# Weight sums of the second FFN tied to its steps, two buffers for modulation rows, x's copies in two parts

## The chip, the cores and the metric

The kernel runs on one core of a Trainium2 chip. The metric is the device time of one execution in microseconds (us). TensorE (PE in the profile) multiplies matrices, VectorE (DVE) and ScalarE (ACT) work on tiles elementwise, GpSimd (POOL) helps with a few, and SyncE (SP) issues nearly all transfers (DMAs) from one queue that is worked through in order. Each engine takes its instructions in the order in which the program was laid out.

## The reference

One layer of a hybrid model on 512 tokens of width 1024, in float32. Three updates of x follow one another, each behind a norm that is scaled and shifted by rows computed from c:

```python
mod = jax.nn.silu(c) @ w_ada + b_ada
sh1, sc1, g1, sh2, sc2, g2, sh3, sc3, g3 = split(mod, 9)
u = rms_norm(x, ffn1_norm_g) * (1 + sc1) + sh1
x = x + 0.5 * g1 * swiglu(u, ffn1_w_in, ffn1_w_out)
u = rms_norm(x, mix_norm_g) * (1 + sc2) + sh2
...                     # mLSTM branch y_a, forgetting attention y_b, from u @ w_mix
merged = sigmoid(g_a) * (y_a @ w_branch_a) + sigmoid(g_b) * (y_b @ w_branch_b)
x = x + g2 * (merged @ w_out)
u = rms_norm(x, ffn2_norm_g) * (1 + sc3) + sh3
x = x + 0.5 * g3 * swiglu(u, ffn2_w_in, ffn2_w_out)
```

`swiglu(u, w_in, w_out)` is `(silu(a) * b) @ w_out` with `a, b` the halves of `u @ w_in`; the inner width is 2816. The change touches the update by `w_out`, the third norm, and the second FFN.

## The kernel before

**Splitting.** Every product is made of three matmuls (`mm3`, lines 108 to 110): each factor is split into a high part (line 89, on ACT) and a low part (line 91, on DVE). A weight tile is fetched into one of three `raw` buffers (`raw`, line 79, on SP), then split into one of four `wh` and four `wl` buffers. A buffer comes free when PE has used it, so weights are fetched and split a few tiles ahead of PE.

**The update by w_out.** `token_gemm` runs twice, once for each half of the 1024 columns, over four blocks of 128 tokens (0 to 3) and four slices of `w_out`. The first slices are multiplied for all blocks, the last two or three slices block by block, so that the blocks end one after another. `residual` gives each finished block to DVE: line 571 multiplies it by the modulation row, line 573 adds it to x, and line 209 (ACT) sums its squares. The modulation row is a tile of 128 x 512, fetched by `mod_bcast` (line 316) from a row in DRAM to all partitions; its tag `gb` has one buffer, so that the second half's row can be fetched only when the first half's last block is through.

**The third norm.** `norm_half` works on two token blocks at a time. `xnorm` (lines 229 to 237) makes the reciprocal root in ten small DVE instructions (lines 125 to 135), scales x, then PE transposes the tiles (line 260), and `u_from` (lines 245 to 247) makes the input of the next product. In the second half of the update, the norm of blocks 0 and 1 is written just ahead of block 3's matmuls, so that PE has block 2 and block 3 to do while the norm's small steps run. The same code, with the same tail of three slices, makes the second norm after the first FFN; there nothing else of a later stage lies beside it.

**The second FFN.** `ffn_in` goes through 22 columns j of 128 (columns 0 and 1 in `ffn_in_halves`, each in two halves of 256 tokens). A column takes two weight tiles. Its result is made by `pair_h`: SiLU on ACT (line 366), a multiply on DVE (line 372 for an even column, 378 for an odd one), and for each pair of columns some sums that serve a product of two-by-two blocks with seven products in place of eight. The weights of the second product need sums too. `pair_weights` makes them: 22 units, each a quarter of the pair's weights, loaded by two DMAs (line 425, tile `s`), four subtractions of 128 x 256 on DVE (lines 430 to 433), and a store to DRAM (line 435, `ws`). There are two tiles: one of tag `st` for even units, and for odd units the buffer that the last pair's `A1` will take. A unit's load, sums and store are written in three successive steps; a column has two steps, one between its two weight tiles and one at its end. An even unit and the odd unit behind it start every three steps. `pair_out` then multiplies, fetching `ws` again.

**What sets the order.** The program is written in the order of the stages, but a planner lays out each engine's instructions: it runs through the program on a clock of its own, and takes, among the instructions whose inputs and buffers are then ready, the one written first. An instruction can so land far ahead of its place when its inputs are early. `issue_after(i)` adds no wait: it only forbids that the instructions inside be placed ahead of `i` on that engine. The loads of `pair_weights` depend on nothing but a free buffer.

**Copies of x.** At the beginning of the second FFN eight DMAs (line 1271) copy x's eight tiles to DRAM (`x3_d`; the profile shows the name `x_d`), since the tiles' memory is used by the pairs. `pair_out` loads them again for the last update.

Of the kernel before, what the change touches and what calls it, by code (L numbers as in the profile page):

```python
# [11 lines left out]
F32 = mybir.dt.float32  # L12
# [8 lines left out]
P = 128  # L21
T = 512
NT = 4
D = 1024
# [19 lines left out]
MUL, ADD, SUB, MAX, MIN = ALU.mult, ALU.add, ALU.subtract, ALU.max, ALU.min  # L44


class Layer:
# [28 lines left out]
    def raw(self, shape, dmas):  # L76
        t = self.wp.tile(shape, F32, name=self.nm("raw"), tag="raw", bufs=3)
        for dst, src in dmas:
            self.nc.sync.dma_start(dst(t), src)
        return t  # L80

    def split(self, src, shape):
# [229 lines left out]
        return G, sh  # L312

    def mod_bcast(self, v, half, pool):
        t = pool.tile([P, 512], F32, name=self.nm("gb"), tag="gb", bufs=1)
        self.nc.sync.dma_start(t, self.mod_d[v:v + 1, half * 512:(half + 1) * 512].to_broadcast([P, 512]))
        return t

# [40 lines left out]
    def pair_h(self, ps_a, ps_b, j, c0, c1, hp, tp):  # L359


        nc = self.nc
        i, w, h0 = j // 2, c1 - c0, c0 // 256
        nh = w // 256
        s = self.tmp(tp, "sl")
        nc.scalar.activation(s[:, :w], ps_a[:, c0:c1], AF.Silu)
        hv = lambda t: t.rearrange("p (h t) -> p h t", t=256)
        if j % 2 == 0:
            if h0 == 0:

                self.E = tp.tile([P, 4, 256], F32, name=self.nm("E"), tag="E", bufs=1)
            nc.vector.tensor_tensor(self.E[:, 0:4:3, :] if nh == 2 else self.E[:, 3 * h0:3 * h0 + 1, :],
                                    hv(ps_b[:, c0:c1]), hv(s[:, :w]), op=MUL)
            return
        if h0 == 0:
            self.Ra[i], self.Rb[i] = self.pair_rest(i, hp, F32)
        Ra, Rb = self.Ra[i], self.Rb[i]
        nc.vector.tensor_tensor(Ra[:, h0:h0 + nh, :], hv(ps_b[:, c0:c1]), hv(s[:, :w]), op=MUL)
        if c1 < T:
            return  # L380
        E, V = self.E, nc.vector.tensor_tensor
        A1 = self.A1[i] = hp.tile([P, 6, 256], F32R, name=self.nm("A1"), tag=f"A{i}", bufs=1)
        V(E[:, 1, :], E[:, 3, :], Ra[:, 1, :], op=ADD)
        V(E[:, 2, :], E[:, 1, :], E[:, 0, :], op=SUB)
        nc.scalar.activation(A1[:, 0:3, :], E[:, 0:3, :], AF.Copy)
        V(A1[:, 3:6, :], E[:, 0:3, :], A1[:, 0:3, :], op=SUB)
        V(Rb[:, 0, :], E[:, 0, :], E[:, 3, :], op=SUB)
        V(Rb[:, 1, :], Ra[:, 0, :], E[:, 2, :], op=SUB)
# [22 lines left out]
    def pair_weights(self, w, hp, tp):  # L411


        nc = self.nc
        V = nc.vector.tensor_tensor
        NP = NJ // 2
        self.ws = [self.dp.tile([P, 4, 512], F32, name=self.nm("ws")) for i in range(NP)]
        ts = {}
        def load(u):
            i, c = u // 2, slice(u % 2 * 256, u % 2 * 256 + 256)  # L420

            t = ts[u] = hp.tile([P, 5, 256], F32, name=self.nm("s"), tag=f"A{NP - 1}", bufs=1) if u % 2 else                 tp.tile([P, 5, 256], F32, name=self.nm("s"), tag="st", bufs=1)
            for n in range(2):
                r = (2 * i + n) * P
                nc.sync.dma_start(t[:, 2 * n:2 * n + 2, :], w[r:r + P, :].rearrange("p (h n) -> p h n", h=2)[:, :, c])
        def sums(u):

            t = ts[u]
            s = lambda n: t[:, n, :]
            V(s(4), s(3), s(1), op=SUB)  # L430
            V(s(1), s(1), s(0), op=SUB)
            V(s(3), s(3), s(1), op=SUB)
            V(s(2), s(2), s(3), op=SUB)
        def store(u):
            nc.sync.dma_start(self.ws[u // 2][:, :, u % 2 * 256:u % 2 * 256 + 256], ts.pop(u)[:, 1:5, :])
        for h in range(3 * NP + 1):
            m, r = h // 3, h % 3
            for u, n in ((2 * m, r), (2 * m + 1, r - 1), (2 * m - 1, r + 2)):
                if 0 <= u < 2 * NP and 0 <= n < 3:
                    (load, sums, store)[n](u)  # L440
            yield
# [663 lines left out]
    def run(self):  # L1105
        nc, tc, A = self.nc, self.tc, self.A
# [2 lines left out]
        self.h_d = self.dp.tile([T, D], F32, name="h_d")  # L1109
        self.g_d = [self.dp.tile([P, T], F32, name=f"g_d{i}") for i in range(2 * NK)]  # L1110

        self.ntmp, self.xn_tiles, self.ffn_act = 5, self.xn_start, self.ffn_h
        with tc.tile_pool(name="f1t", bufs=1) as tp:
            self.consts(tp)
            with tc.tile_pool(name="st", bufs=1) as st:
# [114 lines left out]
                self.dump(f"ya_{m}", self.ya[m])  # L1230
                self.dump(f"yb_{m}", self.yb[m])

        self.ntmp, self.xn_tiles = 4, self.xn_branch
        with tc.tile_pool(name="br", bufs=1) as bp:
            self.mh = [bp.tile([P, T], F32R, name=f"mh{m}") for m in range(NK)]
            self.ml = [bp.tile([P, T], F32R, name=f"ml{m}") for m in range(NK)]

            sg = [bp.tile([P, T], F32, name=self.nm("sg"), tag="sg", bufs=2) for _ in range(2)]
            for m in range(2):
                for _ in self.gate(m, 0, None, sg[m]):  # L1240
                    pass
            self.split_y(self.ya, bp)
            ta = []
            for m in range(NK):
                ta.append(self.branch(m, 0, bp, yp.tile([P, T], F32, name=self.nm("ta"), tag="qk", bufs=16), sg[m] if m < 2 else None))
            self.split_y(self.yb, bp)
            for m in range(NK):
                t = self.branch(m, 1, bp, None)
                nc.gpsimd.tensor_tensor(t, t, ta[m], op=ADD)
                nc.scalar.activation(self.mh[m], t, AF.Copy)  # L1250
                nc.vector.tensor_tensor(self.ml[m], t, self.mh[m], op=SUB)
            self.x_tiles()
            self.x_load(self.x_d)
            lhs = lambda k: (self.mh[k], self.ml[k])
            self.ss_tile()
            self.token_gemm(lhs, NK, A["w_out"][0], 0, self.residual(0.5, 5, 0, bp))
            G3, sh3 = self.mod_cols(6, gain(R_N3))
            self.token_gemm(lhs, NK, A["w_out"][0], 1, self.residual(0.5, 5, 1, bp), 3, None,
                            lambda: self.norm_half(0, bp, G3, sh3))
            self.norm_half(1, bp, G3, sh3)  # L1260
# [4 lines left out]
        with tc.tile_pool(name="f2t", bufs=1) as tp, tc.tile_pool(name="f2h", bufs=1) as hp:  # L1265
            for k in range(NK):
                self.dump(f"u3_{k}", self.uh[k].bitcast(F32))
            x3 = self.dp.tile([T, D], F32, name="x3_d")
            for tb in range(NT):
                for h in range(2):  # L1270
                    nc.sync.dma_start(x3[tb * P:(tb + 1) * P, h * 512:(h + 1) * 512], self.x[tb][h])
            self.ffn_in_halves(A["ffn2_w_in"][0], 2, hp, tp)
            pw = self.pair_weights(A["ffn2_w_out"][0], hp, tp)
            step = lambda *_: next(pw, None)
            self.ffn_in(A["ffn2_w_in"][0], 2, hp, tp, step, step)
            for _ in pw:
                pass
            self.pair_out(A["ffn2_w_out"][0], 8, hp, tp, lambda: self.x_load(x3))


# [28 lines left out]
```

## Time and profile before

| | us |
|---|---|
| median of 3 runs | 1358.96 |
| lowest, highest | 1358.12, 1361.02 |
| the profiled execution | 1359.13 |
| its span | 1357.4 |
| PE busy | 1331.2 (98%) |
| DVE busy | 893.2 (66%) |
| ACT busy | 588.4 (43%) |

The stages around the change, in the profiled execution: the branches' last products end at 949.9; the update by `w_out` runs from there to 1002.8, with its second half from 972.6; the second FFN's first product follows, and the last column's multiply is at 1245.7; the second product runs to the end.

A line of a timeline gives the start and the duration in us, the engine, the line of the kernel, the operation, the tiles written and read, the shapes, the count, and in brackets for how long the engine stood idle before it and what ended that. A line of the waits gives the waiting engine, tile and line, what it waited for, the sum in us, the number of waits and the longest. A line of the windows gives a stretch, its length, busy time and instruction count of PE, PE's weight loads, DVE, ACT and POOL, then PE's granted clock (1.00 is full), the transfers' share and their rate in GB/s.

### The profile page before, as it was taken

How to read it: one execution, taken by the hardware profiler on the slowest of the kernel's cores; microseconds unless marked ns; L12 is line 12 of the kernel's file. 1: busy time of each engine (PE TensorE's matmuls, PEld its weight loads, DVE VectorE, ACT ScalarE, POOL GpSimd, SP SyncE). 2: the span in 40 equal slices, each digit the busy share in tenths (PEclk: the TensorE clock that was granted, in tenths of full speed). 3: DMA queues.
4: the chain of work that ended last, by engine and by line, in shares of the span. 5: the costliest groups of instructions: out<-in, count | busy, mean ns of one | idle time of the engine just before them, and what ended most of it. 6: DMA issues, size and time to landing. Idle time of an engine off the chain costs nothing.

```text
span 1357.4 us, 17796 instructions
## 1 busy us (share of the span) xinstructions
PE 1331.2 (98%) x6520; PEld 1116.0 (82%) x6520; DVE 893.2 (66%) x1661; ACT 588.4 (43%) x978; POOL 46.1 (3%) x71
## 2 busy tenths in 40 slices
PE   7999999999999999999999999999999999999997
PEld 6788887887889888988888888888788888888886
DVE  6866666656558777986686876446577655434776
ACT  4532333313236755556565675333253222323642
POOL 2000000000011101000000000002010000000000
PEclk9999999999999999999999999999989999999999
DMA  9676556666534424444243442464558875434575
GB/s 288 188 224 189 179 184 202 217 194 201 187 86 107 131 85 136 123 116 132 59 140 89 132 129 77 117 198 142 177 170 258 262 229 176 123 93 140 168 249 164
DMA packets 245691, 219.30 MB, mean 162 GB/s; under 512 B 12706, under 2 KB 206914, under 8 KB 245604
## 3 DMA queue, kind: packets, MB, share of 16 engines
q1 hardware_dynamic: 245124, 218.09, 53.6%
q8 instruction: 51, 0.84, 0.2%
q14 instruction: 36, 0.29, 0.1%
q0 software_dynamic: 416, 0.06, 0.0%
q10 hardware_dynamic: 64, 0.02, 0.0%
HBM read 194.47 MB, written 23.66 MB: 161 GB/s over the span
## 4 chain that ended last, share of the span: by engine, by line
PE 88%; DVE 6%; ACT 3%; DMA 2%; issue 1%; SPq 0%; DVEq 0%; ACTq 0%
PE g L110 23%; PE g L108 23%; PE g L109 23%; PE t L110 4%; PE t L108 4%; PE t L109 4%; PE g L693 2%; PE t L1037 2%; PE t L1007 1%; DVE wl L91 1%; DMA s<-in_ffn_w_out_dram 1%; PE t L978 1%; PE t L979 1%; PE t L693 1%; DVE fq L957 1%
## 5 line engine op out<-in xcount | busy, mean ns | idle before, releaser
L89 ACT ACTIVATE wh<-raw 128x1024 fp32r<-128x1024 f32 x236 | 244.3, 1039 | 401.5 <-PE g L109 141.7
L91 DVE TENSOR_TENSOR wl<-raw,wh 128x1024 fp32r<-128x1024 f32 x236 | 289.6, 1229 | 164.4 <-ACT wh L89 147.7
L108 PE MATMUL g<-uh,wh 128*128 128x512 f32 (+2 forms) x984 | 370.3, 377 | 0.5 <-ACT wh L89 0.5
L110 PE MATMUL g<-uh,wl 128*128 128x512 f32 (+2 forms) x984 | 369.4, 376 | 1.1 <-DVE wl L91 1.1
L109 PE MATMUL g<-ul,wh 128*128 128x512 f32 (+2 forms) x984 | 369.3, 376 | 0.0
L110 PEld LDWEIGHTS g<-uh,wl 128*128 128x128 f32 (+1 forms) x984 | 184.7, 188 | 35.7 <-DVE wl L91 1.7
L108 PEld LDWEIGHTS g<-uh,wh 128*128 128x128 f32 (+1 forms) x984 | 184.7, 188 | 33.9 <-ACT wh L89 0.9
L109 PEld LDWEIGHTS g<-ul,wh 128*128 128x128 f32 (+1 forms) x984 | 184.9, 188 | 33.1 <-POOL ul L247 0.2
L108 PE MATMUL g<-wh,uh 128*128 128x512 f32 (+1 forms) x320 | 111.9, 350 | 0.0
L110 PE MATMUL g<-wh,ul 128*128 128x512 f32 (+1 forms) x320 | 111.1, 347 | 0.0
L109 PE MATMUL g<-wl,uh 128*128 128x512 f32 (+1 forms) x320 | 111.0, 347 | 0.0
L284 DVE SCALAR_TENSOR_TENSOR acc<-raw,ccol,acc 128x1024 f32<-128x1024 f32 x49 | 62.8, 1282 | 13.0 <-DMA raw<-in_w_ada_dram 12.2
L108 PEld LDWEIGHTS g<-wh,uh 128*128 128x128 f32 x320 | 60.5, 189 | 7.8 <-DVE tk L892 0.5
L110 PEld LDWEIGHTS g<-wh,ul 128*128 128x128 f32 x320 | 60.5, 189 | 7.8
L109 PEld LDWEIGHTS g<-wl,uh 128*128 128x128 f32 x320 | 60.5, 189 | 7.3
L430 DVE TENSOR_TENSOR s<-s 128x256 f32<-128x256 f32 x22 | 9.3, 425 | 62.8 <-DMA s<-in_ffn_w_out_dram 53.3
L108 PE MATMUL g<-yh,wh 128*128 128x512 f32 x128 | 50.4, 394 | 0.0
L110 PE MATMUL g<-yh,wl 128*128 128x512 f32 x128 | 50.2, 392 | 0.0
L109 PE MATMUL g<-yl,wh 128*128 128x512 f32 x128 | 49.7, 388 | 0.0
L989 ACT ACTIVATE S<-S,mn 128x128 f32<-128x128 f32 (+1 forms) x64 | 35.6, 558 | 18.5 <-DVE mn L981 9.5
L108 PE MATMUL g<-wh,hh 128*128 128x512 f32 x88 | 35.0, 398 | 0.0
L110 PE MATMUL g<-wh,hl 128*128 128x512 f32 x88 | 34.9, 397 | 0.0
(319 smaller groups left out, 2087.1 us busy)
## 6 DMA issues: line engine op xcount, KB each, us to landing
raw<-in_ffn_w_in_dram SPq DMA_DIRECT2D x82, 512.0 KB
raw<-in_w_ada_dram SPq DMA_DIRECT2D x56, 512.0 KB
raw<-in_w_mix_dram SPq DMA_DIRECT2D x48, 512.0 KB
raw<-in_ffn_w_out_dram SPq DMA_DIRECT2D x33, 512.0 KB
s<-in_ffn_w_out_dram SPq DMA_DIRECT2D x44, 256.0 KB
ws<-s SPq DMA_DIRECT2D x22, 512.0 KB
ar<-in_w_ada_dram SPq DMA_DIRECT2D x32, 256.0 KB
raw<-in_w_mix_dram SPq DMA_DIRECT2D x32, 256.0 KB
```

The lines of the kernel that those rows point to most:

```text
L89: nc.scalar.activation(hi, src, AF.Copy)
L91: nc.vector.tensor_tensor(lo, src, hi, op=SUB)
L108: mm(ps, lh, rh, start=start, stop=False)
L109: mm(ps, lh, rl, start=False, stop=False)
L110: self.last_mm = mm(ps, ll, rh, start=False, stop=stop)
L284: nc.vector.scalar_tensor_tensor(acc, r, self.ccol[:, k:k + 1], acc, op0=MUL, op1=ADD)
L693: mm = nc.tensor.matmul(acc_ps[b], (wl if p == 1 else wh)[:, b % 2, s], self.ul[k] if p == 2 else self.uh[k], start=k == 0 and p == 0, sto ...
L957: nc.vector.scalar_tensor_tensor(lo, b[own, :], gc[own, :], d[own, :], op0=MUL, op1=SUB)
L978: nc.tensor.matmul(ps[:, :w], q[:, s], k[:, :w], start=True, stop=False)
L979: nc.tensor.matmul(ps[:, :w], q[:, s], kl[:, :w], start=False, stop=True)
L989: nc.scalar.activation(S[:, ws], S[:, ws], AF.Exp, scale=-1.0, bias=m, accum_out=sm[:, qb:qb + 1])
L1037: nc.tensor.matmul(po[:, q0:], vt[:, kb, i, :], Px[:, o:o + T - q0], start=n == 1, stop=n == 8)
```

## The change

It has three parts.

1. In `pair_weights` the two loads of a unit are placed behind the last weight load written before them (`last_raw`, noted by `raw`) on SP, and the four subtractions behind the last multiply of a column written before them (`last_mul`, noted by `pair_h`) on DVE.
2. The modulation rows of the update by `w_out` take the tag `sg`, whose two buffers the branches use before; the tag `gb` no longer exists in that stage. The first FFN keeps `gb` with one buffer.
3. The four copies of x's left half are written behind the first half of the update, the other four where all eight were.

```diff
@@ raw
-            self.nc.sync.dma_start(dst(t), src)
+            self.last_raw = self.nc.sync.dma_start(dst(t), src)
@@ mod_bcast
-        t = pool.tile([P, 512], F32, name=self.nm("gb"), tag="gb", bufs=1)
+        tag, n = self.gb_tag
+        t = pool.tile([P, 512], F32, name=self.nm("gb"), tag=tag, bufs=n)
@@ pair_h
-            nc.vector.tensor_tensor(self.E[:, 0:4:3, :] if nh == 2 else self.E[:, 3 * h0:3 * h0 + 1, :],
+            self.last_mul = nc.vector.tensor_tensor(self.E[:, 0:4:3, :] if nh == 2 else self.E[:, 3 * h0:3 * h0 + 1, :],
...
-        nc.vector.tensor_tensor(Ra[:, h0:h0 + nh, :], hv(ps_b[:, c0:c1]), hv(s[:, :w]), op=MUL)
+        self.last_mul = nc.vector.tensor_tensor(Ra[:, h0:h0 + nh, :], hv(ps_b[:, c0:c1]), hv(s[:, :w]), op=MUL)
@@ pair_weights
-                nc.sync.dma_start(t[:, 2 * n:2 * n + 2, :], w[r:r + P, :].rearrange("p (h n) -> p h n", h=2)[:, :, c])
+                with self.tc.issue_after(self.last_raw.ins):
+                    nc.sync.dma_start(t[:, 2 * n:2 * n + 2, :], w[r:r + P, :].rearrange("p (h n) -> p h n", h=2)[:, :, c])
...
-            V(s(4), s(3), s(1), op=SUB)
-            V(s(1), s(1), s(0), op=SUB)
-            V(s(3), s(3), s(1), op=SUB)
-            V(s(2), s(2), s(3), op=SUB)
+            with self.tc.issue_after(self.last_mul.ins):
+                V(s(4), s(3), s(1), op=SUB)
+                V(s(1), s(1), s(0), op=SUB)
+                V(s(3), s(3), s(1), op=SUB)
+                V(s(2), s(2), s(3), op=SUB)
@@ run
-        self.ntmp, self.xn_tiles, self.ffn_act = 5, self.xn_start, self.ffn_h
+        self.ntmp, self.xn_tiles, self.ffn_act, self.gb_tag = 5, self.xn_start, self.ffn_h, ("gb", 1)
...
-        self.ntmp, self.xn_tiles = 4, self.xn_branch
+        self.ntmp, self.xn_tiles, self.gb_tag = 4, self.xn_branch, ("sg", 2)
...
             self.token_gemm(lhs, NK, A["w_out"][0], 0, self.residual(0.5, 5, 0, bp))
+            self.x3_d = self.dp.tile([T, D], F32, name="x3_d")
+            def x_spill(h):
+                for tb in range(NT):
+                    nc.sync.dma_start(self.x3_d[tb * P:(tb + 1) * P, h * 512:(h + 1) * 512], self.x[tb][h])
+            x_spill(0)
...
-            x3 = self.dp.tile([T, D], F32, name="x3_d")
-            for tb in range(NT):
-                for h in range(2):
-                    nc.sync.dma_start(x3[tb * P:(tb + 1) * P, h * 512:(h + 1) * 512], self.x[tb][h])
+            x_spill(1)
...
-            self.pair_out(A["ffn2_w_out"][0], 8, hp, tp, lambda: self.x_load(x3))
+            self.pair_out(A["ffn2_w_out"][0], 8, hp, tp, lambda: self.x_load(self.x3_d))
```

## The prediction

> **What bounds the kernel now.** I read the page's busy times first, then what TensorE (PE) waited for, then VectorE (DVE) and PE in order of time where the longest late wait lies.
>
> ```profile
> span 1357.4 us, 17796 instructions
> PE 1331.2 (98%) x6520; PEld 1116.0 (82%) x6520; DVE 893.2 (66%) x1661; ACT 588.4 (43%) x978; POOL 46.1 (3%) x71
> ```
> ```profile
> PE t L178 <- DMA rowsC<-in_b_ada_dram: 5.8, 1, 5.8
> PE g L693 <- ACT uh L658: 5.6, 8, 1.4
> PE t L260 <- DVE xn L236: 3.0, 1, 3.0
> ```
>
> PE is the bound: it idles 1357.4 - 1331.2 = 26.2 us. The first two waits belong to the start of the kernel, which the diff does not touch. The third, 3.0 us, is the only long one after it: PE stands before the transposes of the third norm. No edit here can gain more than that wait and what hangs on it. The work around it, first DVE, then PE:
>
> ```profile
> 972.88 0.42 DVE L430 TENSOR_TENSOR s<-s 128x256 f32<-128x256 f32 x1 [4.57 <-DMA s<-in_ffn_w_out_dram]
> 983.53 0.69 DVE L571 SCALAR_TENSOR_TENSOR rs<-g,gb 128x512 f32<-128x512 f32 x1 [2.46 <-DMA gb<-mod_d]
> 987.55 0.42 DVE L430 TENSOR_TENSOR s<-s 128x256 f32<-128x256 f32 x1 [3.33 <-DMA s<-in_ffn_w_out_dram]
> ...
> 989.75 0.68 DVE L571 SCALAR_TENSOR_TENSOR rs<-g,gb 128x512 f32<-128x512 f32 x1
> 990.46 0.69 DVE L573 TENSOR_TENSOR x<-x,rs 128x512 f32<-128x512 f32 x1
> 992.01 0.16 DVE L230 SCALAR_TENSOR_TENSOR v<-ss,v 128x2 f32<-128x2 f32 x1 [0.85 <-ACT rs L209]
> 994.19 0.49 DVE L236 TENSOR_SCALAR xn<-x,rq 128x512 f32<-128x512 f32 x1
> ```
> ```profile
> 986.43 0.40 PE L110 MATMUL g<-wh,ml 128*128 128x512 f32 x1
> ...
> 990.63 0.40 PE L110 MATMUL g<-wh,ml 128*128 128x512 f32 x1
> ...
> 991.33 0.39 PE L110 MATMUL g<-wh,ml 128*128 128x512 f32 x1
> 994.73 1.11 PE L260 MATMUL t<-ident,xn 128*128 128x128 f32 x4 [3.01 <-DVE xn L236]
> ```
>
> What the reader is to see: PE finishes block 1 of w_out's second half at 986.43 + 0.40 = 986.83. DVE could take its update (L571) at once, but stands at L430, the first weight sum of an FFN that has not begun, until that sum's slice lands at 987.55. Sums and older updates go first, so block 1's update starts at 989.75, 2.9 us late. From its second step (990.46) to the transposes (994.73) the chain is 4.27 us without a hole: square on ACT, rsqrt steps from 992.01, xn at 994.19. PE has three matmuls of block 3 after block 2 and then nothing.
>
> The gap has a second price. The windows of one microsecond, whose column after POOL is the granted clock:
>
> ```profile
> 993.00:994.00 1.00, 0.00 (x0) 0.00 (x0) 0.83 (x6) 0.00 (x0) 0.00 (x0) 0.85 0.30 111
> 994.00:995.00 1.00, 0.27 (x1) 0.27 (x2) 0.96 (x3) 0.81 (x2) 0.00 (x0) 0.50 0.20 20
> 999.00:1000.00 1.00, 1.00 (x5) 0.81 (x4) 1.00 (x3) 1.00 (x4) 0.12 (x1) 0.50 0.00 0
> 1000.00:1001.00 1.00, 1.00 (x5) 0.82 (x4) 1.00 (x4) 1.00 (x3) 0.73 (x1) 0.73 0.00 0
> 1001.00:1002.00 1.00, 1.00 (x6) 0.81 (x5) 1.00 (x4) 1.00 (x3) 0.85 (x1) 1.00 0.00 0
> ```
>
> From 994.73 to 1000 PE works at half clock and loses 5.27 x 0.50 = 2.6 us, in the next microsecond 0.27: 2.9 us. Idle and clock together cost 5.9 us.
>
> **The change part by part.**
>
> *Sums tied behind their own steps on DVE* (L430 to L433). 22 units of four subtractions stay, but none can be issued before the last multiply of the second FFN that was written ahead of it. The first sum so falls behind FFN 2's third column, after the whole stage above. In that stage DVE then has nothing of L430 before block 1's update: L571 at 986.83 + 0.03, L573 0.71 later (989.75 to 990.46) at 987.57, transposes 4.27 later at 991.84. PE is done with its three matmuls at 991.72. Idle 0.1 us in place of 3.0. A gain of 2.9, and with no gap the clock should hold: 2.9 more, 5.8 at most.
>
> A check from the kernel itself: the second norm, after the first FFN's update, runs the same code without sums beside it. Its update of block 1, its transposes and the transposes of its other half, with the last row for the third norm:
>
> ```profile
> 392.25 0.69 DVE L571 SCALAR_TENSOR_TENSOR rs<-g,gb 128x512 f32<-128x512 f32 x1 [2.78 <-PE g L110]
> ...
> 397.19 0.66 PE L260 MATMUL t<-ident,xn 128*128 128x128 f32 x4
> ...
> 412.23 1.94 PE L260 MATMUL t<-ident,xn 128*128 128x128 f32 x16
> ...
> 1011.97 1.94 PE L260 MATMUL t<-ident,xn 128*128 128x128 f32 x16
> ```
> ```profile
> 397.00:398.00 1.00, 0.93 (x7) 0.69 (x6) 1.00 (x3) 1.00 (x2) 0.00 (x0) 1.00 0.00 0
> ```
>
> There the clock is 1.00 through the transposes. From block 1's sum being ready to the other half's transposes the twin takes 412.23 - 392.25 = 19.98 us; here it is 1011.97 - 986.86 = 25.11. The difference is 5.1. Between 5.1 and 5.8 I take 5.1, because the twin holds the small waits that a denser DVE brings.
>
> [...]
>
> *Where the sums go, and what they cost there.* FFN 2's columns come 10.89 us apart:
>
> ```profile
> 1169.60 0.69 DVE L372 TENSOR_TENSOR E<-g,sl 128x512 f32<-128x512 f32 x1 [3.36 <-PE g L110]
> 1180.49 0.69 DVE L378 TENSOR_TENSOR Ra<-g,sl 128x512 f32<-128x512 f32 x1 [3.37 <-PE g L110]
> ```
> ```profile
> 1133.06 0.43 DVE L430 TENSOR_TENSOR s<-s 128x256 f32<-128x256 f32 x1 [3.55 <-DMA s<-in_ffn_w_out_dram]
> 1144.78 0.43 DVE L430 TENSOR_TENSOR s<-s 128x256 f32<-128x256 f32 x1 [6.58 <-DMA s<-in_ffn_w_out_dram]
> ```
> ```profile
> 1025.00:1060.00 35.00, 35.00 (x168) 29.49 (x167) 22.73 (x42) 10.85 (x13) 0.00 (x0) 1.00 0.89 273
> ```
> ```profile
> DVE s L430 <- DMA s<-in_ffn_w_out_dram: 37.9, 12, 7.1
> ```
>
> One buffer needs 1144.78 - 1133.06 = 11.7 us from one unit's sums to the next (store, load, sums). A buffer comes round every three steps, two steps to a column, so its ties lie one and two columns apart in turn: 10.9 and 21.8 us. In the long turn nothing waits; in the short one DVE may wait 11.7 - 10.9 = 0.8 us for the slice. Eleven such waits make some 9 us, against the 37.9 us (longest 7.1) that DVE waits at L430 from 1025 to 1245 today, during which PE is 35.00 of 35.00 us busy in the fullest window. What is queued behind a waiting sum is the split of a weight (L91). Its slack:
>
> ```profile
> 1174.80 1.06 ACT L89 ACTIVATE wh<-raw 128x1024 fp32r<-128x1024 f32 x1 [4.38 <-PE g L109]
> 1175.90 1.23 DVE L91 TENSOR_TENSOR wl<-raw,wh 128x1024 fp32r<-128x1024 f32 x1 [4.01 <-ACT wh L89]
> ```
>
> The split starts when PE leaves one of four weight buffers and is done 2.33 us later (1177.13); three other weights of 10.89 / 2 = 5.44 us lie ahead, so DVE may be late by 16.3 - 2.3 = 14.0 us before PE feels it. Cost zero, bounds 0 and the rival below.
>
> *Loads tied on SP* (L425, two of 256 KB a unit, and the store L435 behind its sums). The same 44 loads and 22 stores are issued, each behind a weight load of FFN 2. They leave the stretch of the third norm and go past FFN 2's weight loads, with the slack just named. The last sums now come behind the multiply four columns before the last one:
>
> ```profile
> 1202.25 0.69 DVE L378 TENSOR_TENSOR Ra<-g,sl 128x512 f32<-128x512 f32 x1 [3.37 <-PE g L110]
> ...
> 1245.70 0.69 DVE L378 TENSOR_TENSOR Ra<-g,sl 128x512 f32<-128x512 f32 x1 [2.06 <-PE g L110]
> ```
> ```profile
> 1215.82 0.43 SPq L79 DMA_DIRECT2D raw<-ws  x1
> ```
>
> So at 1202, before the first read of the summed weights (1215.82, which wants the first unit only) and before the last pair at 1245.70 takes the odd units' buffer. Cost zero.
>
> *Modulation rows in two buffers* (L316, tag "sg"). The second row now need not wait for the first; the 2.46 us wait at 983.53 goes. It alone is worth nothing: that update was through by 985, ahead of block 1's end at 986.83. Both rows now take buffers that the branches hold:
>
> ```profile
> 953.23 0.68 DVE L1251 TENSOR_TENSOR ml<-sg,mh 128x512 fp32r<-128x512 f32 x1
> 964.10 0.69 DVE L571 SCALAR_TENSOR_TENSOR rs<-t,gb 128x512 f32<-128x512 f32 x1 [0.48 <-PE t L110]
> 977.40 0.87 SPq L316 DMA_DIRECT2D gb<-mod_d  x1
> ```
>
> Such a row takes 983.53 - 977.40 = 6.1 us to land at worst. The last branch frees its buffer at 953.91, so even that one lands by 960, ahead of the first use at 964.10. Zero, and up to the 4 us of margin could be lost if SP is held.
>
> *x's copies in two parts* (L1271). Eight transfers as before, the first four merely written earlier; they become ready only with the updates, and PE waits for none of them. Zero.
>
> *Sum.* 1357.4 - 5.1 = 1352.3 us of span. The profiled execution took 1359.13, 1.73 around its span, and the median is 1358.96, 0.17 less: 1352.3 + 1.73 - 0.17 = 1353.9 us, a gain of 0.38%.
>
> **The rivals.**
>
> *The hole stays.* The planner lays the order anew, and block 2's update may land ahead of the small rsqrt steps. Block 2 ends at 990.63 + 0.40 = 991.03; its two steps of 0.71 end at 992.45, the rsqrt steps and xn start then instead of at 987.57 + 992.01 - 990.46 = 989.12, and the transposes 994.73 - 992.01 = 2.72 later, at 995.2: an idle gap of 3.4 us and the half clock again. Nothing is gained: 1359. Against it: the twin has its block 2 update behind the first xn. Chance 0.10.
>
> *The clock falls anyway.* If half clock belonged to the sparse transposes and not to the gap, only the 2.9 us of idle come back: 1356.1. The twin's clock of 1.00 speaks against it. Chance 0.03. [...]
>
> *The late sums starve PE.* DVE waits at L430, behind its multiply, with weight splits behind it; from 14.0 us late PE idles, and a gap like today's costs 5.9 us with its clock. Two of them, less the gain of 5.1, give 1358.96 + 11.8 - 5.1 = 1365.7, slower. It decides where a wait at L430 passes 14 us, or several pile up within one column; for it: the sums' whole load moves into the one stretch with transfers at a share of 0.89, and each chain store, load, sums starts from a multiply. Against: the longest such wait today is 7.1 us. Chance 0.15.
>
> **How the numbers follow.** Forecast 0.72, clock rival 0.03, no gain 0.10, starved 0.15. A measurement of this kernel tells about 0.2%, 2.7 us (its runs spread over 2.9). Faster by more: 0.72 + 0.03 = 0.75; within: 0.10; slower: 0.15. The forecast's own range is 1353.0 to 1355.5. For eight in ten it reaches over the clock rival to the case without gain: 1352.8 (the 5.8 ceiling and 0.3 of spread) to 1359.4.
>
> **What would show it.** Right: no L430 before the first 128x512 multiply of FFN 2; PE's wait at L260 under 0.5 us; clock 1.00 from transposes to FFN 2; the two halves' transposes as far apart as in the twin; waits at L430 short and PE waiting for no wl there; the span's gain all between the w_out matmuls and FFN 2's start. Wrong: a gap before L260 of over 2 us, or PE waiting for wl or wh after 1020.

## The result and the profile after

| | before | after |
|---|---|---|
| median of 8 runs, us | 1358.78 | 1354.65 |
| lowest, highest | 1357.82, 1361.02 | 1354.13, 1357.03 |
| the profiled execution | 1359.13 | 1354.64 |
| its span | 1357.4 | 1352.9 |

The ratio is 0.9972, with a 95% interval from 0.9961 to 0.9983: faster by 4.13 us or 0.3%. The forecast was 1353.9; the kernel takes 0.75 us more. In the new program's line numbers the sums are L434 to L437, their loads L427 and store L439, the update L575 and L577, the column multiplies L373 and L379.

First the page's busy times and the waits of PE, whose columns are those of the table before (sum, number, longest):

```profile
span 1352.9 us, 17800 instructions
PE 1328.6 (98%) x6520; PEld 1113.0 (82%) x6520; DVE 887.8 (66%) x1661; ACT 589.4 (44%) x978; POOL 46.0 (3%) x71
```
```profile
PE g L697 <- ACT uh L662: 5.6, 8, 1.4
PE t L178 <- DMA rowsC<-in_b_ada_dram: 5.6, 1, 5.6
```

The wait of 3.0 us at L260 is gone, and what leads the list now belongs to stages that the change doesn't touch. PE is busy 2.6 us less (1331.2 before) and idle 1352.9 - 1328.6 = 24.3 us, 1.9 less than before. DVE's timeline of the changed kernel through the third norm, with a column multiply far behind it:

```profile
986.98 0.69 DVE L575 SCALAR_TENSOR_TENSOR rs<-g,gb 128x512 f32<-128x512 f32 x1 [2.78 <-PE g L110]
...
991.44 0.49 DVE L236 TENSOR_SCALAR xn<-x,rq 128x512 f32<-128x512 f32 x1
994.82 1.00 DVE L246 TENSOR_SCALAR uf<-t,G,sh 128x256 f32<-128x256 f32 x2 [1.31 <-ACT uh L245]
...
1197.78 0.69 DVE L379 TENSOR_TENSOR Ra<-g,sl 128x512 f32<-128x512 f32 x1 [3.37 <-PE g L110]
```

DVE waits for PE now and not for a slice: block 1's update starts as soon as its sum is there. PE's timeline of the same kernel from the transposes to the second FFN (the 128x256 matmuls are its first), the start of the second FFN in the kernel before, and windows of the changed kernel (PE with the number of its matmuls, its weight loads, DVE, ACT, POOL, granted clock, transfers):

```profile
991.98 0.66 PE L260 MATMUL t<-ident,xn 128*128 128x128 f32 x4
...
996.91 0.39 PE L109 MATMUL g<-wl,mh 128*128 128x512 f32 x1
997.14 0.40 PE L110 MATMUL g<-wh,ml 128*128 128x512 f32 x1
997.37 0.28 PE L108 MATMUL g<-uh,wh 128*128 128x256 f32 x1
997.50 0.28 PE L109 MATMUL g<-ul,wh 128*128 128x256 f32 x1
...
1001.66 0.39 PE L110 MATMUL g<-uh,wl 128*128 128x256 f32 x1 [0.16 <-DVE wl L91]
...
1007.08 1.95 PE L260 MATMUL t<-ident,xn 128*128 128x128 f32 x16
```
```profile
1002.54 0.40 PE L110 MATMUL g<-wh,ml 128*128 128x512 f32 x1
1002.77 0.28 PE L108 MATMUL g<-uh,wh 128*128 128x256 f32 x1
```
```profile
991.00:992.00 1.00, 0.86 (x5) 0.38 (x3) 0.89 (x5) 0.56 (x1) 0.00 (x0) 1.00 0.00 0
995.00:996.00 1.00, 1.00 (x6) 0.77 (x5) 1.00 (x3) 1.00 (x3) 0.10 (x1) 1.00 0.06 21
998.00:999.00 1.00, 1.00 (x11) 1.00 (x10) 1.00 (x3) 1.00 (x2) 0.56 (x1) 1.00 0.00 0
1150.00:1215.00 65.00, 65.00 (x289) 53.81 (x288) 34.33 (x62) 17.92 (x22) 0.00 (x0) 1.00 0.71 216
```

The clock is 1.00 at every place where it was 0.50 (in every window from 990 to 1006). Behind the norm's transposes PE works, up to 997.37, on block 3 of `w_out`, whose matmuls of 128x512 start every 0.23 us (996.91, 997.14); at half clock, in the kernel before, they started 0.42 us apart (999.49, 999.91). The second FFN's first matmul comes at 997.37 in place of 1002.77. In the ten microseconds behind it DVE is the fuller engine, 1.00 busy in every window from 995 to 1004, and PE waits once for a weight's split (1001.66). Further on in the second FFN PE is busy without a hole, though the sums and their transfers have moved there. DVE's waits at the sums and SP's at the stores, between 1020 and 1280:

```profile
DVE s L434 <- DMA s<-in_ffn_w_out_dram: 3.7, 4, 1.8
```
```profile
SPq L439 <- DVE s L437: 45.1, 15, 6.3
```

**Where the time came from.** Set beside the rows of before, the first xn of the norm comes at 991.44 in place of 994.19, 2.75 us earlier. The second FFN's first matmul comes 5.40 us earlier, the transposes of the other half 4.89 (1007.08 in place of 1011.97). The column multiply at 1197.78 stood at 1202.25: 4.47 us earlier, and this distance stays to the end (4.49 between the two profiled executions). So 2.75 us are won ahead of the first xn and 2.65 between it and the second FFN, and 0.93 of that is given back behind its first matmul, which leaves 1.72 us behind the first xn. This last part can be read as one number in any kernel: the stretch from the first xn to that column multiply took 1202.25 - 994.19 = 208.06 us before and takes 1197.78 - 991.44 = 206.34 us now. The experiments below use it, since it leaves out whatever an execution lost earlier.

### The profile page after: what moved, and what is told of

It reads as the page before. It is cut to its first block, busy times and chain, and to the rows that moved or that the text cites. A ratio compares the mean times of both kernels' runs of the same rounds, so it can differ in the third digit from the quotient of the medians.

```text
span 1352.9 us, 17800 instructions
## 1 busy us (share of the span) xinstructions
PE 1328.6 (98%) x6520; PEld 1113.0 (82%) x6520; DVE 887.8 (66%) x1661; ACT 589.4 (44%) x978; POOL 46.0 (3%) x71
## 4 chain that ended last, share of the span: by engine, by line
PE 86%; DVE 7%; ACT 3%; DMA 2%; issue 1%; SPq 0%; DVEq 0%; ACTq 0%
PE g L110 22%; PE g L108 22%; PE g L109 22%; PE t L110 4%; PE t L108 4%; PE t L109 4%; PE g L697 2%; PE t L1041 2%; PE t L1011 1%; DVE wl L91 1%; PE t L982 1%; PE t L983 1%; PE t L697 1%; DVE fq L961 1%; DMA h_d<-hn 1%
## 5 line engine op out<-in xcount | busy, mean ns | idle before, releaser
L108 PE MATMUL t<-wh,hh 128*128 128x512 f32 x88 | 34.8, 396 | 0.0
```

Source lines behind the costliest of these rows:

```text
L108: mm(ps, lh, rh, start=start, stop=False)
```

## The experiments

Four questions: which part of the change carries the gain, whether the sums cost anything where they now stand, what the parts other than the ties do alone, and what the 1.72 us behind the first xn consist of. Ratios are to the kernel before on the same chip.

| kernel | median us | before | ratio, 95% interval |
|---|---|---|---|
| both ties alone | 1355.09 | 1358.61 | 0.9976, 0.9967 to 0.9986 |
| the sums' tie alone | 1354.42 | 1358.61 | 0.9969, 0.9958 to 0.9981 |
| the loads' tie alone | 1355.57 | 1358.61 | 0.9978, 0.9970 to 0.9987 |
| both ties alone, from unit 4 | 1354.47 | 1358.61 | 0.9969, 0.9956 to 0.9981 |
| no ties, the other two parts | 1363.89 | 1358.56 | 1.0036, 1.0022 to 1.0050 |
| the two buffers alone | 1363.31 | 1358.56 | 1.0034, 1.0021 to 1.0048 |
| x's copies in two parts alone | 1358.95 | 1358.56 | 1.0004, 0.9995 to 1.0013 |
| before, with fill | 1359.53 | 1358.56 | 1.0007, 0.9998 to 1.0016 |
| both ties alone, from unit 6 | 1358.79 | 1359.39 | 0.9994, 0.9986 to 1.0003 |
| ties from unit 6, with fill | 1357.86 | 1359.39 | 0.9994, 0.9985 to 1.0003 |
| ties from unit 6, copies in two parts | 1359.04 | 1358.66 | 1.0008, 0.9999 to 1.0016 |
| the sums' tie from unit 6 | 1358.59 | 1358.66 | 0.9995, 0.9987 to 1.0004 |

### The ties, together and one by one

Both ties without the other two parts (against the changed kernel):

```diff
-        self.ntmp, self.xn_tiles, self.gb_tag = 4, self.xn_branch, ("sg", 2)
+        self.ntmp, self.xn_tiles, self.gb_tag = 4, self.xn_branch, ("gb", 1)
-            x_spill(0)
...
-            x_spill(1)
+            for tb in range(NT):
+                for h in range(2):
+                    nc.sync.dma_start(self.x3_d[tb * P:(tb + 1) * P, h * 512:(h + 1) * 512], self.x[tb][h])
```

> Both ties of the weight sums, but the modulation rows in one buffer and x's copies in one part, as before. Theory (the early sums on VectorE are the whole cause): VectorE meets no L430-type sum before block 1's update, the transposes wait for under 0.3 us, the clock stays at 1.00; 1354.7 us, as the full change. Rival (the second buffer for the modulation row carries part of the gain, since block 0's update waited 2.46 us for it): 1355.5 to 1357 us, with a wait for the row ahead of block 1's update.

Measured 1355.09. The interval overlaps that of the whole change almost entirely, so beside the ties the other two parts add nothing that can be told.

The sums' tie alone (against the kernel before; the lines that note the multiply in `pair_h` are left out here):

```diff
-            V(s(4), s(3), s(1), op=SUB)
...
+            with self.tc.issue_after(self.last_mul.ins):
+                V(s(4), s(3), s(1), op=SUB)
...
```

> Only the four subtractions are tied; the loads of the first two units still go out early on SP. Theory (what stands in VectorE's queue is the cause): 1354.7 us, no gap at the third norm. Rival (SP's early loads and stores, standing ahead of weight loads and copies, cost PE as well): at least 1 us of the gain missing, 1355.7 to 1357 us, and a wait of PE for a weight.

The loads' tie alone (against the kernel before; the line that notes the load in `raw` is left out here):

```diff
-                nc.sync.dma_start(t[:, 2 * n:2 * n + 2, :], w[r:r + P, :].rearrange("p (h n) -> p h n", h=2)[:, :, c])
+                with self.tc.issue_after(self.last_raw.ins):
+                    nc.sync.dma_start(t[:, 2 * n:2 * n + 2, :], w[r:r + P, :].rearrange("p (h n) -> p h n", h=2)[:, :, c])
```

> Only the loads are tied; the sums are free but need their slice. Theory: the sums can't be ready before the second FFN and are laid out behind the norm, 1354.7 us. Rival (without the tie on VectorE the sums move ahead of the second FFN's own multiplies and hold weight splits there): a wait of PE for a split in the second FFN and 1356 us or more.

Measured 1354.42 and 1355.57: either tie alone brings nearly all of it. A sum that may not be issued early does no harm, and a sum whose load is issued late isn't taken early by the planner either. The loads' tie is also the test of the rival that starves PE, since it leaves the sums where the planner puts them. DVE's waits at the sums between 1025 and 1245, and the window, in the kernel with the loads' tie alone:

```profile
DVE s L434 <- DMA s<-in_ffn_w_out_dram: 31.6, 13, 4.9
```
```profile
1025.00:1245.00 220.00, 220.00 (x972) 182.17 (x971) 119.25 (x195) 60.60 (x73) 0.00 (x0) 1.00 0.66 200
```

DVE waits 31.6 us for slices, up to 4.9 us at a time, and PE is busy 220.00 of 220.00 us. So it isn't the length of these waits that counts but where they stand; the likely reason is the prediction's slack of 14.0 us for a split. Ahead of 1025 a free sum likely did cost something: one stands on DVE ahead of the norm's second half, with a wait of 0.76 us at 1008.64, and the stretch from the first xn is 206.95 us, 0.6 more than in the changed kernel, in this one execution.

### Units 0 to 3 left free

Both ties hold from unit 4 on, without the other two parts; the first four units, two for each pair of columns and each with half of its weights, are placed as before (against the kernel with both ties alone):

```diff
-                with self.tc.issue_after(self.last_raw.ins):
+                with self.tc.issue_after(self.last_raw.ins) if u >= 4 else nullcontext():
...
-            with self.tc.issue_after(self.last_mul.ins):
+            with self.tc.issue_after(self.last_mul.ins) if u >= 4 else nullcontext():
```

> Units 0 to 3 stay untied, so the sums of units 0 and 2 still stand in the first half of the update by w_out and make VectorE wait there (5.16 and 4.57 us before); from unit 4 on all is tied. Theory (only a wait that ends later than block 1's result reaches PE, and that is unit 4's alone): 1354.7 us, the whole gain. Rival (each early wait costs its share): one of three waits is gone, a third of the gain, about 1357.4 us.

Measured 1354.47. The early waits of DVE at units 0 and 2 (in the kernel before 4.57 us at 972.88, here 4.10) cost nothing that can be told; the gain hangs on the units from 4 on.

### The two other parts without the ties

No ties, but the two buffers and the copies in two parts (against the changed kernel):

```diff
-                with self.tc.issue_after(self.last_raw.ins):
-                    nc.sync.dma_start(t[:, 2 * n:2 * n + 2, :], w[r:r + P, :].rearrange("p (h n) -> p h n", h=2)[:, :, c])
+                nc.sync.dma_start(t[:, 2 * n:2 * n + 2, :], w[r:r + P, :].rearrange("p (h n) -> p h n", h=2)[:, :, c])
...
-            with self.tc.issue_after(self.last_mul.ins):
+            with nullcontext():
```

> The other half of the change: two buffers for the modulation rows and x's copies in two parts, without any tie. VectorE's layout then has unit 4's sums ahead of block 0's update of the second half and unit 6's sums between the small rsqrt steps of the norm. Theory (a sum that waits for its slice holds what stands behind it): the norm's chain waits for unit 6's slice, which came at 997.5 before, so the transposes start near 1001 in place of 994.7; a gap of 5 us or more with half clock behind it, 1361 to 1366 us, slower than before. Rival (these two parts cost nothing, as the prediction has them): 1358 to 1359.5 us.

Then each alone (against the kernel before; in these programs and in that with fill the lines' numbers are shifted by a few). The buffers:

```diff
-        t = pool.tile([P, 512], F32, name=self.nm("gb"), tag="gb", bufs=1)
+        tag, n = self.gb_tag
+        t = pool.tile([P, 512], F32, name=self.nm("gb"), tag=tag, bufs=n)
...
-        self.ntmp, self.xn_tiles = 4, self.xn_branch
+        self.ntmp, self.xn_tiles, self.gb_tag = 4, self.xn_branch, ("sg", 2)
```

> The second buffer for the modulation rows alone, no ties, copies as before. Theory: the row's wait no longer holds back VectorE's planned order, unit 4's and unit 6's sums move up as in the run without ties, and the time is that run's within 1 us (1361 to 1366 us). Rival (the buffer is worth nothing in either direction): 1358 to 1359.5 us.

The copies:

```diff
...
+            x_spill(0)
             G3, sh3 = self.mod_cols(6, gain(R_N3))
...
-            for tb in range(NT):
-                for h in range(2):
-                    nc.sync.dma_start(x3[tb * P:(tb + 1) * P, h * 512:(h + 1) * 512], self.x[tb][h])
+            x_spill(1)
```

> x's copies in two parts alone. VectorE's layout around the third norm is that of the kernel before but for two neighbouring instructions. Theory: the gap of 3 us and the half clock stay, 1358.8 us within 0.7. Rival (the copies, now ahead of weight loads on SP, hold the weights): PE waits for a split and 1360 us or more.

The copies alone change nothing (1358.95). The buffers alone cost 4.75 us (1363.31 against 1358.56), and the two without ties 5.33 (1363.89). DVE's timeline with the buffers alone, and PE at the transposes:

```profile
985.10 0.43 DVE L433 TENSOR_TENSOR s<-s 128x256 f32<-128x256 f32 x1 [4.70 <-DMA s<-in_ffn_w_out_dram]
986.82 0.68 DVE L574 SCALAR_TENSOR_TENSOR rs<-g,gb 128x512 f32<-128x512 f32 x1
...
991.21 0.16 DVE L129 TENSOR_TENSOR rt<-rt,v 128x2 f32<-128x2 f32 x1
995.15 0.42 DVE L433 TENSOR_TENSOR s<-s 128x256 f32<-128x256 f32 x1 [3.78 <-DMA s<-in_ffn_w_out_dram]
995.49 0.16 DVE L130 TENSOR_SCALAR rd<-rt 128x2 f32<-128x2 f32 x1
```
```profile
999.13 1.12 PE L260 MATMUL t<-ident,xn 128*128 128x128 f32 x4 [5.51 <-DVE xn L236]
```

The order on DVE is another one. Unit 4's sums (here L433) stand ahead of block 0's update instead of behind its first step, and unit 6's between two of the small rsqrt steps (L129 and L130), where DVE stands 3.78 us for a slice of a later stage. PE's gap is 5.5 us. A buffer that removes a wait of 2.46 us made the kernel slower by what it did to the order. That the planner hoists the sums because its own clock no longer waits for the second row is the likely reading; only the order itself is shown.

### What stands behind the first xn: fill

The fill puts 26 transposes of the identity, which nobody reads, between block 2's last matmul and the norm's transposes, so that PE doesn't fall idle (against the kernel before):

```diff
-    def norm_half(self, hf, pool, G, sh):
+    def norm_half(self, hf, pool, G, sh, fill=0):
...
+        if fill:
+            with self.tc.issue_after(self.last_mm.ins):
+                for i in range(fill):
+                    nc.tensor.transpose(b[0][:, 0:P], self.ident, self.ident)
...
-                            lambda: self.norm_half(0, bp, G3, sh3))
+                            lambda: self.norm_half(0, bp, G3, sh3, 26))
```

> The kernel before, with 26 extra transposes of the identity put behind block 2's last matmul (about 3 us of PE work that nobody reads). The sums stay where they were, so the norm's chain is as late as before and the gap is as long, but PE is kept at work in it. Theory (half clock comes from the gap): the clock stays at 1.00 through the transposes, and about 1.5 to 2.5 us of the half clock's price come back: 1356.3 to 1357.5 us. Rival (the clock falls at the transposes anyway): clock 0.50 for some 5 us as before and 1358.8 to 1359.8 us.

Measured 1359.53: nothing gained. The fill's windows, where the kernel before had 0.50 after its gap, and its DVE timeline:

```profile
994.00:995.00 1.00, 0.33 (x1) 0.14 (x1) 1.00 (x4) 0.85 (x2) 0.00 (x0) 1.00 0.73 207
996.00:997.00 1.00, 1.00 (x11) 0.96 (x10) 0.31 (x1) 1.00 (x4) 0.00 (x0) 1.00 0.67 230
```
```profile
993.51 0.49 DVE L236 TENSOR_SCALAR xn<-x,rq 128x512 f32<-128x512 f32 x1
996.69 0.42 DVE L434 TENSOR_TENSOR s<-s 128x256 f32<-128x256 f32 x1 [1.09 <-DMA s<-in_ffn_w_out_dram]
998.41 0.99 DVE L246 TENSOR_SCALAR uf<-t,G,sh 128x256 f32<-128x256 f32 x2
...
1201.83 0.69 DVE L382 TENSOR_TENSOR Ra<-g,sl 128x512 f32<-128x512 f32 x1 [3.37 <-PE g L110]
```

With the fill PE waits 0.46 and 0.66 us here and the clock holds at 1.00; before, it waited 3.01 us and the clock fell to 0.50. So the theory that PE's idleness takes the clock away stands. But the time doesn't come back: the stretch from the first xn is 1201.83 - 993.51 = 208.32 us, no shorter than before. Two things are different besides the clock. On PE all 18 matmuls of block 3 now stand behind the transposes, where the kernel before has three ahead of them and two between. On DVE all four of unit 6's sums, which wait for their slice, stand ahead of the u-steps (L246), where the kernel before has three; the u-steps start 4.90 us after xn in place of 3.38 in the changed kernel. A second theory follows: two delays lie side by side behind the first xn, PE at half clock and unit 6's sums on DVE, and taking either away alone shows little.

### Unit 6's sums away, the gap kept

The next four take only unit 6's sums away from the norm and leave unit 4's, so that the gap before the transposes stays. Ties from unit 6 (against the kernel with both ties alone):

```diff
-                with self.tc.issue_after(self.last_raw.ins):
+                with self.tc.issue_after(self.last_raw.ins) if u >= 6 else nullcontext():
...
-            with self.tc.issue_after(self.last_mul.ins):
+            with self.tc.issue_after(self.last_mul.ins) if u >= 6 else nullcontext():
```

> Ties on units 6 and later only; units 0 to 5 are free as before, so that unit 4's sum still stands ahead of block 1's update, while unit 6's sums leave the place ahead of the u-steps (before: 997.55 to 998.81). Both theories expect the gap of 3.0 us at the third norm's transposes and half clock behind it, as before. Theory now held (what sets the time after the gap is DVE's chain; unit 6's sums and the half clock both delay it, one under the other): the u-steps then wait for the transposes at half clock and start 0 to 0.6 us earlier than before's 998.81; the time is 1358.0 to 1358.8. Rival (unit 6's sums alone carried the part that the idle time did not): 1.3 us less than before, 1357.3.

The same with the fill shown above:

> The same ties, with 26 transposes of the identity, read by nobody, behind block 2's last matmul as in the kernel with fill: unit 4's sum still makes DVE late, but PE stays busy and the clock at 1.00. Theory now held: with unit 6's sums out of the way the u-steps start 3.4 us after the first xn, as in the changed kernel, 1.2 to 1.4 us earlier than before, and the time is 1357.0 to 1357.5, so the clock has a price of about 1 us that neither the fill nor the ties alone would show. Rival (the half clock is hidden behind DVE altogether): no less than the kernel with the same ties and no fill. Rival (the prediction's term, 2.9 us): 1355.7.

The medians of the two are 1358.79 and 1357.86, the first within the 1358.0 to 1358.8 of the theory then held, the second above its 1357.0 to 1357.5. Set beside the ties from unit 4, the first also shows which sums carry the gain: with units 4 and 5 tied the ratio is 0.9969, at most 0.9981, and with them free 0.9994, at least 0.9986.

In the profiled execution of the first the clock did something that neither theory expected. PE's timeline, a window, and DVE's timeline, with the ties from unit 6:

```profile
996.04 0.66 PE L260 MATMUL t<-ident,xn 128*128 128x128 f32 x4 [2.92 <-DVE xn L236]
```
```profile
996.00:997.00 1.00, 0.96 (x6) 0.69 (x6) 1.00 (x3) 0.83 (x2) 0.00 (x0) 1.00 0.00 0
```
```profile
995.50 0.48 DVE L236 TENSOR_SCALAR xn<-x,rq 128x512 f32<-128x512 f32 x1
998.88 1.00 DVE L246 TENSOR_SCALAR uf<-t,G,sh 128x256 f32<-128x256 f32 x2 [1.31 <-ACT uh L245]
...
1201.84 0.69 DVE L379 TENSOR_TENSOR Ra<-g,sl 128x512 f32<-128x512 f32 x1 [3.37 <-PE g L110]
```

PE idled 2.92 us and the clock stayed at 1.00. The stretch is 1201.84 - 995.50 = 206.34 us, that of the changed kernel. With the fill, whose first xn is at 992.94 and whose column multiply is at 1199.76, it is 206.82. To see the price of the half clock without unit 6's sums, an execution was wanted in which the clock does fall; two kernels with the same order on DVE were run for that. One adds the copies in two parts to the ties from unit 6 (the edit of the copies above); the other drops the loads' tie:

```diff
-                with self.tc.issue_after(self.last_raw.ins) if u >= 6 else nullcontext():
+                with nullcontext():
```

> Ties on units 6 and later, and x's copies in two parts (which alone changed nothing): DVE's order at the norm is that of the kernel with the ties from 6, with its gap of 2.9 us before the third norm's transposes and no sums ahead of the u-steps. From the first xn of the third norm to the column multiply near 1200, the kernel before takes 208.06 us, the changed kernel 206.34, and the kernel with the ties from 6, whose clock stayed at 1.00 in its profiled execution in spite of the gap, 206.34. If the clock falls behind the gap this time, the stretch tells what half clock costs with unit 6's sums out of the way: 206.3 to 206.6 if DVE hides it, 209.2 if it adds the prediction's 2.9 us, between if part of it counts. If the clock does not fall, 206.3 again. Time 1356 to 1359.

> Only the sums of units 6 and later tied, all loads free. The same order on DVE at the norm, the same gap of 2.9 us. The stretch from the first xn to the column multiply near 1200: 206.3 to 206.6 with the clock at 1.00, or with half clock hidden by DVE; up to 209.2 if half clock counts in full. Time 1356 to 1359.

In both the clock fell. The one with the copies, PE, two windows and DVE:

```profile
996.53 1.11 PE L260 MATMUL t<-ident,xn 128*128 128x128 f32 x4 [3.36 <-DVE xn L236]
...
1004.40 0.28 PE L108 MATMUL g<-uh,wh 128*128 128x256 f32 x1
```
```profile
995.00:996.00 1.00, 0.00 (x0) 0.00 (x0) 0.83 (x6) 0.02 (x1) 0.00 (x0) 0.58 0.08 27
1001.00:1002.00 1.00, 1.00 (x4) 0.81 (x3) 1.00 (x3) 1.00 (x3) 0.51 (x1) 0.51 0.00 0
```
```profile
995.98 0.49 DVE L236 TENSOR_SCALAR xn<-x,rq 128x512 f32<-128x512 f32 x1
1000.41 1.00 DVE L246 TENSOR_SCALAR uf<-t,G,sh 128x256 f32<-128x256 f32 x2 [2.35 <-ACT uh L245]
...
1203.71 0.69 DVE L379 TENSOR_TENSOR Ra<-g,sl 128x512 f32<-128x512 f32 x1 [3.37 <-PE g L110]
```

The stretch is 1203.71 - 995.98 = 207.73 us; in the other it is 1203.62 - 995.73 = 207.89. All of them side by side, one execution each, in us from the first xn: to the second FFN's first matmul, to the transposes of the other half, and to the column multiply near 1200.

| | clock | first matmul | transposes | multiply |
|---|---|---|---|---|
| unit 6's sums away: ties from 6 | 1.00 | 5.93 | 15.63 | 206.34 |
| the same, with fill | 1.00 | 7.43 | 15.77 | 206.82 |
| ties from 6, with copies | 0.50 for 6.8 us | 8.42 | 17.05 | 207.73 |
| the sums' tie from 6 | 0.50 for 6.8 us | 8.59 | 17.21 | 207.89 |
| sums in place: fill | 1.00 | 7.44 | 18.55 | 208.32 |
| copies alone | 0.50 for 3.4 us | 7.54 | 17.24 | 207.53 |
| before | 0.50 for 6.8 us | 8.58 | 17.78 | 208.06 |

Up to the second FFN the half clock counts and the sums don't. Without the sums PE gets there 2.49 to 2.66 us later at half clock (8.42 and 8.59 against 5.93), and the sums change nothing (8.58 before; 7.44 against 7.43 with fill). Behind that point DVE counts. At full clock PE comes early, and the way from the first matmul to the transposes, which wait for DVE's xn, takes 9.70 us; when PE comes late by the half clock it takes 8.62 or 8.63. PE's holes on this way end behind steps of DVE: in the changed kernel behind the last u-step (done at 999.88), a weight's split (done at 1001.61) and the xn (from 1006.45). So about 1.1 us of the loss comes back, and at the multiply the half clock costs 1.39 to 1.55. The sums stand in DVE's way just there: with fill, at full clock, the transposes come 2.78 us later and the multiply 1.50; at half clock the sums cost 0.17 to 0.33 at the multiply. Both together cost 208.06 - 206.34 = 1.72, not 3.0: a late PE gives DVE time for its sums, and a late DVE makes an early PE of less use.

The fill has a price of its own, 1.50 us at the first matmul and 0.48 at the multiply (ties from 6 with and without it). It therefore doesn't show the clock's price alone, and what the sums cost at full clock without fill wasn't run. The medians fit this picture: neither the fill alone nor the ties from 6 without it show anything (ratios 1.0007, 0.9994, 1.0008 and 0.9995, each interval holds 1). The pair with ties from 6 and fill should by its stretch be 1.2 us faster than before; its interval, 0.9985 to 1.0003, can't confirm that. No variant is measurably faster than the changed kernel.

## Why the prediction was right, and where not

- *PE waits at L260 because DVE stands at L430 ahead of block 1's update; without it, transposes at 991.84 and 0.1 us of idle time.* Right: 991.98, and no wait at L260. The first xn comes 2.75 us earlier, against 2.9 forecast; the changed kernel's execution reaches block 1's update 0.12 us later than the forecast's 986.86.
- *With no gap the clock holds, 2.9 us more; of both together 5.1 by the twin.* The clock held, and up to the second FFN the price was about right: its first matmul comes 2.65 us earlier behind the first xn (5.93 in place of 8.58), in all 5.40, between the twin's 5.1 and the windows' 5.8. The step that was too large is what the prediction put behind that point: "the span's gain all between the w_out matmuls and FFN 2's start". It put the loss there at nothing, and the runs show 0.93 us given back, since PE, coming early, meets DVE's pace. The half clock alone costs 1.39 to 1.55 us at the multiply. A second delay behind the first xn the prediction never priced: unit 6's sums, 1.50 us alone with fill. Together the two cost 1.72. The twin gave a better total than the windows (5.1 and not 5.8) because its measure ends at the other half's transposes, behind a part of what is given back. By this measure the changed kernel takes 1007.08 - 986.98 = 20.10 us against the twin's 19.98 and 25.11 before: 5.01 won there, and not all of it kept.
- *The sum, 5.1.* The profiled executions differ by 4.49 us: 0.15 less than forecast up to the first xn (2.75 for 2.9), and 1.72 in place of 2.2 behind it. That the total came this near is in part the luck of having taken the twin's figure. The medians differ by 4.13; the last 0.36 us lies within the spread of 3 us among executions of one kernel, and what makes it wasn't looked for.
- *The sums in the second FFN cost nothing.* Right. DVE waits 3.7 us there between 1020 and 1280, less than the 9 us estimated, and even 31.6 us of such waits between 1025 and 1245, with the loads' tie alone, left PE without a hole. The rival that starves PE didn't occur.
- *The loads and stores on SP cost nothing.* Right, though SP stands 45.1 us before the stores.
- *The two buffers: zero.* Right only together with the ties. Alone they cost 4.75 us. The prediction asked whether the row would land in time, and not what the planner does with the order once a wait is gone.
- *The copies: zero.* Right, 1358.95 against 1358.56.
- *The hole stays; the clock falls anyway.* Neither occurred: block 2's update stands behind the first xn, as the forecast had it, and the clock held through the sparse transposes.

## What to carry to other kernels

An instruction that waited for a transfer of a later stage cost here by what was queued behind it on its engine: such waits were worth 4 us at the third norm, and nothing in the second FFN's columns (31.6 us of them, PE 220.00 of 220.00 us busy), so one looks for the place, not for the sum of the waits. Two delays behind one point didn't add up here (1.72 us, not 3.0); price each with the other taken away, and read a stretch between two fixed instructions rather than the whole time. When a planner lays out the order, freeing a buffer or a wait can hoist other work into a worse place, so a part that is harmless beside a tie has to be tried without it too.

## What the runs showed of the hardware

Gaps of nearly equal length did different things to the clock. With 3.01 us of idle time (before), 2.82 (copies alone), 2.90 (the sums' tie from 6) and 3.36 (ties from 6 with copies) the clock fell; with 2.92 (ties from 6) it didn't. And it fell at different moments and for different lengths. The windows of the kernel with the copies alone, whose transposes begin at 994.62:

```profile
995.00:996.00 1.00, 1.00 (x9) 0.70 (x8) 1.00 (x3) 0.41 (x1) 0.00 (x0) 1.00 0.76 243
996.00:997.00 1.00, 1.00 (x8) 1.00 (x7) 0.16 (x1) 0.75 (x3) 0.00 (x0) 0.57 0.60 200
997.00:998.00 1.00, 1.00 (x6) 1.00 (x5) 0.57 (x2) 1.00 (x3) 0.00 (x0) 0.50 0.75 262
998.00:999.00 1.00, 1.00 (x3) 0.76 (x3) 0.97 (x3) 0.79 (x2) 0.00 (x0) 0.50 0.04 6
999.00:1000.00 1.00, 1.00 (x5) 0.76 (x4) 1.00 (x4) 0.77 (x2) 0.28 (x1) 0.72 0.03 10
```

Here PE worked at full clock for 1.5 us before the fall (the 0.57 from 996 taken as 1.00 and then 0.50). The clock lost 0.43 + 0.50 + 0.50 + 0.28 = 1.71 us, which at half clock is a stay of 3.42 us. Before the change the clock fell with PE still idle (0.85 in the window from 993, less than 2.3 us after PE stopped at 991.72), and the windows from 993 to 1001 add up to 3.42 us lost, a stay of 6.84, twice as long. In three other executions in which the clock fell behind a gap at the norm it lost 3.41 or 3.42 us too (ties from 6 with copies, the sums' tie from 6, the two buffers alone); without ties the mean clock of 0.90 from 990 to 1025 makes it about 3.5. Where PE was still idle at the fall (before, and in those three: 0.00 busy in the window of the fall, with a clock of 0.58 to 0.85), the stay was 6.8 us; where it was at work, with the copies alone, 3.42. What sets the moment of the fall and the length of the stay wasn't shown.

The clock also fell at the start of the kernel. In the profiled execution with the ties from 6 it was at 0.50 from 12 to 15, and lost 1.70 us from 11 to 16; before the change it was 1.00 there:

```profile
12.00:13.00 1.00, 1.00 (x7) 1.00 (x7) 0.83 (x7) 0.64 (x2) 0.00 (x0) 0.50 1.20 298
```

That execution reached the norm 1.31 us later than the one before the change (first xn at 995.50 against 994.19), though its program differs only from unit 6's loads on. Two others with such a stay at the start (1.71 us lost from 12 to 16 in each), ties from 6 with copies and the sums' tie from 6, have their first xn at 995.98 and 995.73. A part of the spread among executions of one kernel then likely comes from such stays; a stretch that begins behind it is steadier: 206.34, 206.37, 206.35 and 206.36 us in the changed kernel, both ties alone, the sums' tie alone and both ties from unit 4.
